# Weights split ahead: an even spread over the feed-forward slots, and 14 more chunks, in a two-layer flow block

## The chip, the cores and the metric

The kernel runs on one core of a Trainium2 chip. The metric is the device time of one execution in microseconds (us); times of runs are given as the median. The core's engines are TensorE (PE, with its weight loads as PEld), VectorE (DVE), ScalarE (ACT), GpSimd (POOL) and SyncE (SP). Each runs its own instructions in order. DMA transfers are issued from the queues of SP, ACT and POOL.

## What is computed

Two layers of a hybrid backbone over 256 context tokens and 256 latent tokens, 1024 channels wide, all in float32. Each layer is a half-step SwiGLU feed-forward network, four token mixers in parallel (a convolution, a gated linear recurrence, a gated delta net, windowed attention), merged by gates and projected, and a second half-step feed-forward network. Only the latent tokens are an output, so the last layer's end runs on the latent half alone.

```python
def swiglu(h, w_gate_up, w_down):
    g, u = jnp.split(h @ w_gate_up, 2, axis=-1)
    return (jax.nn.silu(g) * u) @ w_down
...
# every sub-layer: h = LN(x)*(1+scale)+shift, scale/shift/gate from SiLU(c) @ ada_w
# x <- LayerNorm(alpha*x + w*gate*f(h)),  w = 1/2 for the feed-forward networks
# mixer: z = h @ w_in, four branches, merged = sum(sigmoid(gate_b) * proj_b(y_b)), f = merged @ w_out
```

## The kernel before, in words

**Products in three parts.** Tokens are handled in four tiles of 128 (tiles 0 and 1 context, 2 and 3 latent). A float32 product is made of three PE matmuls, since each operand is split into a rounded part (hi) and a rest (lo): hi by hi (L427), hi by lo (L428), lo by hi (L429), in `mm3`. Weights come in chunks of 128 x 1024 floats (512 KB). `chunk` loads one on SP's queue into `wr` (two buffers), ACT casts it to hi (L123), and DVE or POOL subtracts to get lo (L124; two of three on DVE in a full feed-forward network, all on DVE at the second mixer's end and in the last network). hi and lo go to `wh` and `wl` (three buffers each) or to a named spot: `F`, `Y`, `B` are slots that hold both parts, `G` is four units of 512 columns. `pair` loads two chunks by one transfer (tile `raw`).

**Stages.** In us from the span's start: layer 0 first network about 40 to 440, layer 0 mixer to 1230, layer 0 second network to 1645, layer 1 first network to 2030, layer 1 mixer to about 2545, the norms behind it to 2566, the last network (latent tiles only) to 2749, the last norm and the output to the end at 2766. In what follows the networks are called F0a, F0b, F1a and F1b.

**Fill slots.** `ffn` takes a list `fill`: after most steps of its loops one entry is popped and called, some 25 times in a network; the rest is called ahead of the last stage. Two kinds of work stand in these lists:
- steps of the modulation product (`ada_dot`): a 1 MB load `wa` on SP and four DVE products of 1024 columns (tile `junk`, L203); 28 steps in F0a, 24 in F0b, 12 in F1a;
- weights split ahead (`presplit`): for 38 chunks of the second layer's `w_in`, two halves each: load `C` on SP (L136), cast on ACT (L138), store on ACT's queue, subtraction on DVE (tile `T`, L140), store on POOL's queue (L141). The parts go to a DRAM tile `pre`, and `z_chunk` loads them from there in the mixer, so that the mixer has no cast and no subtraction for them. 14 chunks are done in F0b, 24 in F1a.

`both` lays the two lists over each other, one entry of each to a slot; the shorter gets empty places at its front.

**The second mixer's end.** `mixer` merges the branches, then multiplies by `w_out` (8 chunks, names `wo`; each is used by tile 2 and by tile 3). `SPOT` says where each chunk's parts stand. `fetch` takes chunks 0 to 3 during the merges and 4 to 7 behind the load of `x` from `xspill`. Then each of the two tiles has a chain of two norms: residual (L574, L576), centre (L272, L273, squares on ACT L278, L280), norm (L419, L420), a second centre, ACT L291, PE transposes (L303), modulation, and a split to `h` (L159, L161). F1b's first three pairs of chunks (names `f1`, spots `LAT`) are fetched and split while this goes on.

A scheduler orders the instructions of each engine by priorities and expected times; `issue_after` ties an instruction to follow another.

## Time and profile before

| what | us |
| --- | --- |
| median of three runs | 2767.25 (2759.94 to 2774.62) |
| the profiled execution's own time | 2767.44 |
| its span | 2765.7 |
| PE busy | 2597.6 (94%) |
| DVE busy | 1920.4 (69%) |
| ACT busy | 1094.4 (40%) |
| POOL busy | 883.3 (32%) |

The time is the device's for the whole execution; the span is from the first to the last instruction that the profiler saw, and 1.7 us lie around it. Busy shares are means over the span. An engine's idle time is put down to what ended it.

### The profile page before, as it was taken

The page shows a single profiled execution, that of the slowest core. Times are in us where ns is not written, and L with a number is a line of the kernel's source. Part 1 is how long each engine was busy: PE and PEld are TensorE (multiplying, and loading weights), DVE is VectorE, ACT ScalarE, POOL GpSimd, SP SyncE. Part 2 cuts the span into 40 slices and gives each one's busy share as a digit, 9 for nine tenths or more (in the row PEclk, how much of TensorE's full clock was granted, in tenths as well). Part 3 has the DMA queues.
Part 4 walks back from the last instruction along what each step waited for, and adds up shares of the span by engine and source line. Part 5 has one row for each costly group of instructions (what it writes and reads, how often), then busy time and mean ns, then how long its engine had stood idle before and what let it go on. Part 6 is the DMA issues. An engine that isn't in the chain of part 4 may idle for free.

```text
span 2765.7 us, 38791 instructions
## 1 busy us (share of the span) xinstructions
PE 2597.6 (94%) x14534; PEld 2169.8 (78%) x14534; DVE 1920.4 (69%) x3181; ACT 1094.4 (40%) x2016; POOL 883.3 (32%) x697
## 2 busy tenths in 40 slices
PE   7999999998998999999999989999999989888998
PEld 4877778777776787878778888878887877787897
DVE  4795966678999744266869464758667899756455
ACT  3222245473332533354322353332434534444443
POOL 1323223224545434434233343333210056411221
PEclk9999999999999999999999999999999999999999
DMA  7564633245323433438855449865464754357353
GB/s 268 197 212 154 211 120 104 62 138 168 103 85 96 137 118 124 159 109 312 303 207 191 122 167 329 317 203 171 139 228 136 242 175 149 117 164 257 128 183 107
DMA packets 194779, 477.80 MB, mean 173 GB/s; under 512 B 32816, under 2 KB 72976, under 8 KB 192544
## 3 DMA queue, kind: packets, MB, share of 16 engines
q1 hardware_dynamic: 173216, 424.39, 46.5%
q10 hardware_dynamic: 15264, 30.95, 3.1%
q0 software_dynamic: 6112, 19.99, 1.8%
q8 instruction: 114, 1.87, 0.3%
q14 instruction: 73, 0.60, 0.1%
HBM read 401.82 MB, written 73.45 MB: 172 GB/s over the span
## 4 chain that ended last, share of the span: by engine, by line
PE 32%; DVE 9%; DMA 8%; issue 3%; ACT 3%; POOL 1%; SPq 0%; ACTq 0%; DVEq 0%; POOLq 0%
PE pm L429 9%; PE pm L428 9%; PE pm L427 9%; DMA C<-in_win_dram 4%; DVE junk L203 2%; DVE wl L124 1%; DVE T L140 1%; DMA wr<-in_f_dram 1%; DMA wr<-in_wo_dram 1%; PE pg L921 1%; DMA wa<-in_adaw_dram 1%; PE px L429 1%; PE px L428 1%; PE px L427 1%; DVE G L912 1%
## 5 line engine op out<-in xcount | busy, mean ns | idle before, releaser
L427 PE MATMUL pm<-h,wh 128*128 128x512 f32 (+1 forms) x2512 | 899.9, 360 | 24.9 <-ACT h L159 10.7
L429 PE MATMUL pm<-h,wl 128*128 128x512 f32 (+1 forms) x2512 | 896.4, 357 | 19.4 <-DVE wl L124 18.7
L428 PE MATMUL pm<-h,wh 128*128 128x512 f32 (+1 forms) x2512 | 896.5, 357 | 6.3 <-POOL h L161 6.3
L123 ACT CAST wh<-wr 128x1024 fp32r<-128x1024 f32 x304 | 318.8, 1049 | 621.8 <-DMA wr<-in_f_dram 202.7
L427 PEld LDWEIGHTS pm<-h,wh 128*128 128x128 f32 x2512 | 481.4, 192 | 103.9 <-ACT h L159 12.1
L429 PEld LDWEIGHTS pm<-h,wl 128*128 128x128 f32 x2512 | 481.6, 192 | 98.4 <-DVE wl L124 25.0
L428 PEld LDWEIGHTS pm<-h,wh 128*128 128x128 f32 x2512 | 482.0, 192 | 78.7 <-POOL h L161 8.0
L124 POOL TENSOR_TENSOR wl<-wr,wh 128x1024 fp32r<-128x1024 f32 x108 | 277.4, 2568 | 459.8 <-ACT wh L123 418.6
L124 DVE TENSOR_TENSOR wl<-wr,wh 128x1024 fp32r<-128x1024 f32 x196 | 275.0, 1403 | 209.6 <-ACT wh L123 205.0
L203 DVE SCALAR_TENSOR_TENSOR junk<-wa,cb 128x1024 bf16<-128x1024 f32 x256 | 366.3, 1471 | 10.8 <-DMA wa<-in_adaw_dram 5.7
L161 POOL TENSOR_TENSOR F<-G,F 128x512 fp32r<-128x512 f32 (+1 forms) x94 | 138.0, 1468 | 350.5 <-ACT F L159 336.1
L1155 DVE SCALAR_TENSOR_TENSOR C<-C,vec 128x482 f32<-128x482 f32 (+29 forms) x240 | 173.1, 721 | 4.4 <-ACT C L1147 1.5
L427 PE MATMUL pm<-wh,F 128*128 128x512 f32 x368 | 142.8, 390 | 1.4 <-DVE M L574 1.2
L428 PE MATMUL pm<-wl,F 128*128 128x512 f32 x368 | 143.5, 390 | 0.2 <-POOL wl L124 0.2
L429 PE MATMUL pm<-wh,F 128*128 128x512 f32 x368 | 142.2, 390 | 0.0
L140 DVE TENSOR_TENSOR T<-C,T 128x512 fp32r<-128x512 f32 x76 | 67.1, 883 | 85.7 <-ACT T L138 83.2
L124 DVE TENSOR_TENSOR wl<-raw,wh 128x1024 fp32r<-128x1024 f32 x62 | 76.3, 1232 | 61.6 <-ACT wh L123 61.6
L916 POOL TENSOR_TENSOR wk<-wk,cd 128x512 f32<-128x512 f32 x56 | 72.4, 1295 | 127.8 <-PE pg L938 73.1
L159 ACT CAST F<-G 128x512 fp32r<-128x512 f32 (+1 forms) x94 | 51.0, 543 | 140.0 <-DVE G L441 139.5
L620 DVE SCALAR_TENSOR_TENSOR G<-pm,vec,G 128x506 f32<-128x506 f32 (+5 forms) x126 | 87.4, 694 | 22.3 <-ACT G L615 20.7
L123 ACT CAST wh<-raw 128x1024 fp32r<-128x1024 f32 x64 | 67.1, 1051 | 86.8 <-PE pm L428 40.2
L441 DVE TENSOR_TENSOR G<-G,pm 128x512 f32<-128x512 f32 (+1 forms) x93 | 54.4, 585 | 67.4 <-PE pm L429 63.5
(409 smaller groups left out, 4492.8 us busy)
## 6 DMA issues: line engine op xcount, KB each, us to landing
wr<-in_f_dram SPq DMA_DIRECT2D x204, 512.0 KB, 4.1
wa<-in_adaw_dram SPq DMA_DIRECT2D x64, 1024.0 KB, 5.1
wr<-in_win_dram SPq DMA_DIRECT2D x94, 512.0 KB, 3.6
raw<-in_f_dram SPq DMA_DIRECT2D x30, 1024.0 KB, 5.0
C<-in_win_dram SPq DMA_DIRECT2D x76, 256.0 KB, 4.9
pre<-T ACTq DMA_DIRECT2D x76, 256.0 KB, 4.8
pre<-T POOLq DMA_DIRECT2D x76, 256.0 KB, 5.5
wl<-pre SPq DMA_DIRECT2D x36, 512.0 KB, 5.3
```

Source lines behind the costliest of these rows:

```text
L123: nc.scalar.copy(h, r)
L124: (nc.gpsimd if pool_lo else nc.vector).tensor_sub(l, r, h.bitcast(F32))
L140: nc.vector.tensor_sub(lo, raw, h.bitcast(F32))
L161: eng.tensor_sub(lo, src, hi.bitcast(F32))
L203: nc.vector.scalar_tensor_tensor(junk, w3[:, a], 1.0, self.cb[:, s], op0=ALU.mult, op1=ALU.mult, accum_out=self.modT[l][:, i + a, s:s + 1])
L427: nc.tensor.matmul(ps, wh, xh, start=first, stop=False)
L428: nc.tensor.matmul(ps, wh, xl, start=False, stop=False)
L429: nc.tensor.matmul(ps, wl, xh, start=False, stop=last)
L441: nc.vector.tensor_mul(hf[:, c], sg[:, c], pu[:, c])
L620: nc.vector.scalar_tensor_tensor(acc[:, :, d:], src[:, :, :n - d], w(j), acc[:, :, d:], op0=ALU.mult, op1=ALU.add)
L916: nc.gpsimd.tensor_mul(S(d, n + 1).rearrange("p (h e) -> p h e", h=4), S(d, n).rearrange("p (h e) -> p h e", h=4), gs["cd"][:, d * N_CH + ...
L1155: V.scalar_tensor_tensor(o, x, w(j), o, op0=ALU.mult, op1=ALU.add)
```

## The change

Four things. `both` spreads each list evenly over 25 slots, so a slot gets 0 to 2 modulation steps and 1 to 3 halves. An entry of the split-ahead list is now one half of a chunk (before, a whole chunk); 44 halves are done in F0b (28 before), 60 in F1a (48 before). Each load `C` is tied to come behind the latest `wr` load on SP. And the list has 14 more chunks: the 8 chunks of `w_out` of the second layer and the first 6 of F1b's `f1`. `ready` (which `z_chunk` now calls) loads their parts from DRAM straight into the spots, 1 MB for a chunk in place of the 512 KB of the float32 weights, with no cast and no subtraction. In all 28 halves are added (28 casts, 28 subtractions, 28 loads, 56 stores) and the splits of 14 chunks fall away at the second mixer's end (16 casts and 16 subtractions, since a chunk in `G` has two). F0a's modulation steps, with no split-ahead beside them, are spread by `both` too: three slots get two of them.

```diff
--- before.py
+++ after.py
@@ -44,7 +44,7 @@
 )
 PRE = [Z_GK, Z_GK + 1, Z_GK + 2, Z_GK + 3, Z_AK, Z_AV] + [i for z in (Z_GQ, Z_GV, Z_CG, Z_CA, Z_AQ, Z_LX, Z_LG, Z_GZ)
                                                             for i in range(z, z + 4)]
-PRE_AT = 14
+PRE_AT, SLOTS, N_WO, N_F1 = 44, 25, 8, 3
 LOW = 20000
 SPOT = ("F", "F", "G", "G", "Y", "Y", "B", None)
 LAT = ((None, None), ("F", "F"), ("F", None))
@@ -104,7 +104,7 @@
         self.n_ck += 1
         if raw is None:
             raw = self.sb.tile([P, 1024], F32, tag="wr", bufs=2, name="wr")
-            nc.sync.dma_start(raw, src)
+            self.fetched = nc.sync.dma_start(raw, src).ins
         elif isinstance(raw, str):
             raw = self.slot(raw, name="raw")[:, :1024]
             nc.sync.dma_start(raw, src)
@@ -124,28 +124,33 @@
             (nc.gpsimd if pool_lo else nc.vector).tensor_sub(l, r, h.bitcast(F32))
         return hi, lo
 
-    def presplit(self, l, i):
-        nc = self.nc
-        dst = self.dr.tile([P, 2048], F32, name=f"pre{l}_{i}")
-        self.pre[l, i] = dst
-
-        def go():
-            for k in range(2):
-                c = slice(k * 512, (k + 1) * 512)
-                raw = self.unit("C")
-                nc.sync.dma_start(raw, self.t["win"][l, i][:, c])
-                h, lo = self.T(F32R), self.T(F32R)
-                nc.scalar.copy(h, raw)
-                nc.scalar.dma_start(dst[:, c], h.bitcast(F32))
-                nc.vector.tensor_sub(lo, raw, h.bitcast(F32))
-                nc.gpsimd.dma_start(dst[:, 1024 + k * 512:1024 + (k + 1) * 512], lo.bitcast(F32))
-
-        return go
-
-    def z_chunk(self, l, i, at=None, raw=None):
-        if (l, i) not in self.pre:
-            return self.chunk(self.t["win"][l, i], at=at, raw=raw)
-        nc, src = self.nc, self.pre[l, i]
+    def presplit(self, key, src):
+        nc = self.nc
+        dst = self.dr.tile([P, 2048], F32, name="pre" + "_".join(str(k) for k in key))
+
+        def go(k):
+            c = slice(k * 512, (k + 1) * 512)
+            raw = self.unit("C")
+            with self.tc.issue_after(self.fetched):
+                nc.sync.dma_start(raw, src[:, c])
+            h, lo = self.T(F32R), self.T(F32R)
+            nc.scalar.copy(h, raw)
+            nc.scalar.dma_start(dst[:, c], h.bitcast(F32))
+            nc.vector.tensor_sub(lo, raw, h.bitcast(F32))
+            nc.gpsimd.dma_start(dst[:, 1024 + k * 512:1024 + (k + 1) * 512], lo.bitcast(F32))
+            self.pre[key] = dst
+
+        return [lambda k=k: go(k) for k in range(2)]
+
+    def ready(self, key, src, at=None, raw=None):
+        if key not in self.pre:
+            return self.chunk(src, at=at, raw=raw)
+        nc, src = self.nc, self.pre[key]
+        if at == "G":
+            hl = [self.G(F32R) for _ in range(4)]
+            for k in range(4):
+                nc.sync.dma_start(hl[k].bitcast(F32), src[:, k * 512:(k + 1) * 512])
+            return hl[:2], hl[2:]
         if at:
             w = self.slot(at, F32R, name="w" + at)
             nc.sync.dma_start(w.bitcast(F32), src)
@@ -154,6 +159,9 @@
         nc.sync.dma_start(hi.bitcast(F32), src[:, :1024])
         nc.sync.dma_start(lo.bitcast(F32), src[:, 1024:])
         return hi, lo
+
+    def z_chunk(self, l, i, at=None, raw=None):
+        return self.ready(("win", l, i), self.t["win"][l, i], at, raw)
 
     def split(self, hi, lo, src, pool_lo=True):
         self.last = self.nc.scalar.copy(hi, src).ins
@@ -460,7 +468,9 @@
         self.ju = lambda: self.unit("C")
         chunk = self.chunk
 
-        def two(src, at=(None, None)):
+        def two(src, at=(None, None), key=None):
+            if key and key + (0,) in self.pre:
+                return [self.ready(key + (a,), src[a], at[a]) for a in range(2)]
             if lat:
                 return self.pair(src, "Y", at)
             return [chunk(src[a], at[a]) for a in range(2)]
@@ -473,7 +483,7 @@
                 at = LAT if lat else ((None, None), (None, "Y"), ("Y", "F"))
                 ws = start or []
                 for i in range(0 if start else nh):
-                    ws.append(two(self.t["f1"][l, f, 2 * (m0 + i):2 * (m0 + i) + 2], at[i]))
+                    ws.append(two(self.t["f1"][l, f, 2 * (m0 + i):2 * (m0 + i) + 2], at[i], ("f1", l, f, i)))
                 hid.append((self.F(F32R), self.F(F32R)))
                 for g in groups:
                     if lat:
@@ -1378,7 +1388,7 @@
 
         def fetch(n0, n1):
             for n in range(n0, n1):
-                ws[n] = self.chunk(self.t["wo"][l, n // 4, n % 4], at=spots[n])
+                ws[n] = self.ready(("wo", l, n), self.t["wo"][l, n // 4, n % 4], spots[n])
 
         def conv_out():
             y[0] = self.new_y()
@@ -1480,12 +1490,16 @@
             return box, after
 
         def both(ada, pre):
-            n = max(len(ada), len(pre))
-            ada, pre = ([None] * (n - len(x)) + list(x) for x in (ada, pre))
-            return [lambda fs=fs: [f() for f in fs if f] for fs in zip(ada, pre)]
+            n = SLOTS
+            ada, pre = ([fs[len(fs) * i // n:len(fs) * (i + 1) // n] for i in range(n)] for fs in (ada, pre))
+            return [lambda fs=x + y: [f() for f in fs] for x, y in zip(ada, pre)]
 
         every = (0, 1, 2, 3)
-        pre = [self.presplit(1, i) for i in PRE]
+        L = DEPTH - 1
+        pre = [(("win", L, i), self.t["win"][L, i]) for i in PRE]
+        pre += [(("wo", L, n), self.t["wo"][L, n // 4, n % 4]) for n in range(N_WO)]
+        pre += [(("f1", L, 1, m, a), self.t["f1"][L, 1, 2 * m + a]) for m in range(N_F1) for a in range(2)]
+        pre = [f for k, x in pre for f in self.presplit(k, x)]
         for l in range(DEPTH):
             last = l == DEPTH - 1
 
```

On SP's queue in F0b, at the list's start, loads stand in this order before (`C` is a half to be split ahead, `wr` a chunk that the network needs, `wa` a modulation step's weights):

```order
L136 DMA C<-in_win_dram 128x512
L107 DMA wr<-in_f_dram 128x1024
L136 DMA C<-in_win_dram 128x512
L107 DMA wr<-in_f_dram 128x1024 x3
L136 DMA C<-in_win_dram 128x512 x6
L107 DMA wr<-in_f_dram 128x1024
L136 DMA C<-in_win_dram 128x512 x2
```

and now, from the same transfer of the gate rows on:

```order
L107 DMA wr<-in_f_dram 128x1024 x4
L135 DMA C<-in_win_dram 128x512 x2
L107 DMA wr<-in_f_dram 128x1024 x2
L135 DMA C<-in_win_dram 128x512 x2
L207 DMA wa<-in_adaw_dram 128x2x1024
L107 DMA wr<-in_f_dram 128x1024
L207 DMA wa<-in_adaw_dram 128x2x1024 x2
L107 DMA wr<-in_f_dram 128x1024
```

Before, up to six halves stand in a row there, and now two or three stand behind a `wr`.

On SP's queue at the second mixer's end, from the last two loads ahead of `x`, before:

```order
L107 DMA wr<-in_wo_dram 128x1024
L1423 DMA x<-xspill 128x2048
L107 DMA wr<-in_wo_dram 128x1024 x2
L98 DMA raw<-in_f_dram 128x2x1024
L107 DMA wr<-in_wo_dram 128x1024 x2
L107 DMA wr<-in_f_dram 128x1024 x2
L98 DMA raw<-in_f_dram 128x2x1024 x3
```

and now (`prewo_4` is chunk 4 of `w_out` with both parts, `pref_1_1_0_0` the first chunk of F1b):

```order
L1433 DMA x<-xspill 128x2048
L156 DMA wY<-prewo_4_398 128x2048
L107 DMA wr<-in_f_dram 128x1024
L156 DMA wF<-pref_1_1_1_0_404 128x2048
L156 DMA wY<-prewo_5_399 128x2048
L159 DMA wh<-prewo_7_401 128x1024
L160 DMA wl<-prewo_7_401 128x1024
L98 DMA raw<-in_f_dram 128x2x1024
L159 DMA wh<-pref_1_1_0_0_402 128x1024
L160 DMA wl<-pref_1_1_0_0_402 128x1024
L159 DMA wh<-pref_1_1_0_1_403 128x1024
L156 DMA wB<-prewo_6_400 128x2048
```

Behind `x` there were four chunks of `w_out` (2 MB) with one pair of `f1` (1 MB) between them; now chunk 6 (`wB`) stands behind 7.5 MB of other loads, 8.5 MB from `x` to its own end (the row of `wl` of `pref_1_1_0_1`, 512 KB, stands ahead of it too and is left out here as it repeats).

On DVE at the same place, from the split of chunk 6 to the first norm of tile 2, before:

```order
L124 TENSOR_TENSOR wB<-wr,wB 128x1024
L124 TENSOR_TENSOR wl<-wr,wh 128x1024
L574 TENSOR_TENSOR M<-pm,gate 128x512
L124 TENSOR_TENSOR wl<-raw,wh 128x1024 x2
L576 SCALAR_TENSOR_TENSOR x,sum<-x,M 128x512
L574 TENSOR_TENSOR M<-pm,gate 128x512
L576 SCALAR_TENSOR_TENSOR x,sum<-x,M 128x512
L272 TENSOR_SCALAR ns<-sum 128x1
L273 TENSOR_SCALAR nm<-sum 128x1
L419 SCALAR_TENSOR_TENSOR M<-x,nm,norm_g 128x512 x2
L124 TENSOR_TENSOR wF<-raw,wF 128x1024 x2
L280 TENSOR_SCALAR v<-var 128x1
```

and now:

```order
L584 TENSOR_TENSOR M<-pm,gate 128x512
L586 SCALAR_TENSOR_TENSOR x,sum<-x,M 128x512
L584 TENSOR_TENSOR M<-pm,gate 128x512
L586 SCALAR_TENSOR_TENSOR x,sum<-x,M 128x512
L280 TENSOR_SCALAR ns<-sum 128x1
L281 TENSOR_SCALAR nm<-sum 128x1
L427 SCALAR_TENSOR_TENSOR M<-x,nm,norm_g 128x512 x2
L288 TENSOR_SCALAR v<-var 128x1
```

The subtractions L124 are gone from the norms' chain. (Lines of the kernel after are 8 to 14 higher from here on.) On PE the products by `w_out` are reordered: of the 96 matmuls on the two tiles, the 24 with chunks 6 and 7 stood at two places before (12 in the middle, 12 at the end) and are now the last 24.

## Rows read from the trace of the kernel before

**Rows 1.** The page, part 1: busy us of each engine, share, instructions.
```profile
PE 2597.6 (94%) x14534; PEld 2169.8 (78%) x14534; DVE 1920.4 (69%) x3181; ACT 1094.4 (40%) x2016; POOL 883.3 (32%) x697
```

**Rows 2.** Busy by stretch: us, PE, PEld, DVE, ACT, POOL, PEclk, DMA share, GB/s.
```profile
1250.00:1605.00 355.00, 350.38 (x1591) 286.98 (x1591) 265.93 (x371) 114.46 (x165) 114.50 (x80) 1.00 0.63 218
1645.00:1965.00 320.00, 317.26 (x1428) 259.23 (x1427) 200.03 (x260) 111.87 (x153) 112.55 (x92) 1.00 0.72 246
2545.00:2566.00 21.00, 5.95 (x25) 4.35 (x23) 13.65 (x38) 14.71 (x30) 6.09 (x8) 0.59 0.67 247
```

**Rows 3.** PE's waits in 1250 to 1605 (F0b): total us, times, longest.
```profile
PE pm L429 <- DVE wl L124: 4.2, 4, 1.8
```

**Rows 4.** PE's waits in 1645 to 1965 (F1a).
```profile
PE pm L427 <- DVE M L574: 1.2, 1, 1.2
PE pm L429 <- DVE wl L124: 0.8, 2, 0.5
PE pm L427 <- ACT wh L123: 0.7, 1, 0.7
```

**Rows 5.** PE's waits in 50 to 400 (F0a).
```profile
PE pm L429 <- DVE wl L124: 6.3, 4, 2.8
```

**Rows 6.** PE's waits in 2500 to 2566 (the second mixer's end).
```profile
PE pg L303 <- ACT T L291: 12.7, 2, 9.4
PE pm L427 <- ACT wh L123: 1.8, 2, 1.1
```

**Rows 7.** The page, part 5: split-ahead's subtraction on DVE, its busy and idle time.
```profile
L140 DVE TENSOR_TENSOR T<-C,T 128x512 fp32r<-128x512 f32 x76 | 67.1, 883 | 85.7 <-ACT T L138 83.2
```

**Rows 8.** Groups by line in 1640 to 1820: split-ahead's cast on ACT.
```profile
L138 ACT CAST T<-C 128x512 fp32r<-128x512 f32 x47 | 29.2, 621 | 78.8 <-DMA C<-in_win_dram 73.4 <-DVE T L140 2.5 <-DVE M L574 2.0
```

**Rows 9.** DVE's busy time by stretch in F0b: us, DVE, PEclk, DMA share, GB/s.
```profile
1360.00:1400.00 40.00, 40.00 (x53) 0.96 0.78 276
1440.00:1480.00 40.00, 26.29 (x34) 1.00 0.44 150
```

**Rows 10.** DVE's timeline in F0a: start, us, instruction.
```profile
178.56 1.21 DVE L203 SCALAR_TENSOR_TENSOR junk<-wa,cb 128x1024 bf16<-128x1024 f32 x1
179.70 3.42 DVE L203 SCALAR_TENSOR_TENSOR junk<-wa,cb 128x1024 bf16<-128x1024 f32 x1
```

**Rows 11.** DVE's timeline at the norms behind the second mixer.
```profile
2542.53 2.36 DVE L124 TENSOR_TENSOR wF<-raw,wF 128x1024 fp32r<-128x1024 f32 x2 [0.59 <-ACT wF L123]
...
2548.57 1.22 DVE L124 TENSOR_TENSOR wF<-raw,wF 128x1024 fp32r<-128x1024 f32 x1
...
2550.32 1.23 DVE L124 TENSOR_TENSOR wl<-raw,wh 128x1024 fp32r<-128x1024 f32 x1
2551.45 0.69 DVE L576 SCALAR_TENSOR_TENSOR x<-x,M 128x512 f32<-128x512 f32 x1
```

**Rows 12.** PE's timeline at the same place, [idle before <-releaser].
```profile
2545.34 0.39 PE L428 MATMUL pm<-wl,F 128*128 128x512 f32 x1
2545.57 0.39 PE L429 MATMUL pm<-wh,F 128*128 128x512 f32 x1
2555.31 1.97 PE L303 MATMUL pg<-ident,T 128*128 128x128 f32 x8 [9.35 <-ACT T L291]
2560.64 1.97 PE L303 MATMUL pg<-ident,T 128*128 128x128 f32 x8 [3.36 <-ACT T L291]
```

**Rows 13.** SP's timeline at the same place: issue of the load of `x`.
```profile
2515.49 0.33 SPq L1423 DMA_DIRECT2D x<-xspill  x1
```

**Rows 14.** DMA issues in 2512 to 2548: KB each, us to landing.
```profile
x<-xspill SPq DMA_DIRECT2D x1, 1024.0 KB, 6.0
```

**Rows 15.** Busy by stretch, columns as in rows 2: what the DMA moved.
```profile
20.00:30.00 10.00, 6.53 (x44) 4.01 (x37) 5.46 (x8) 6.15 (x8) 3.41 (x2) 0.66 1.02 419
2515.00:2525.00 10.00, 10.00 (x81) 9.78 (x81) 5.35 (x7) 4.92 (x8) 1.43 (x2) 1.00 0.89 323
```

**Rows 16.** Tile C's users, split-ahead's subtraction: ns min/median/max, first and last start us.
```profile
L140 DVE TENSOR_TENSOR T<-C,T x76: 677/693/3144, 1245.2 to 1816.8; 128x512 fp32r<-128x512 f32 x76
```

## The prediction

> **What bounds the kernel now.** I read the busy shares first. PE is busy 94% of the span, DVE 69%, the others under half [rows 1]. So the question for every edit is whether PE waits less or more, and not how much work DVE or ACT gains. Next I read the stretches that the change touches, one by one. In F0b PE is busy 350.4 of 355 us, in F1a 317.3 of 320; only behind the second mixer is it idle, 15 of 21 us [rows 2]. Then I read what ended PE's waits in each. In F0b it was DVE's lo part of a weight, 4.2 us in four waits [rows 3]; in F1a three small causes, 2.7 us in all [rows 4]; in F0a the lo part again, 6.3 us [rows 5]. At the mixer's end ACT's cast of a weight cost 1.8 us and the norms' ACT L291 12.7 us [rows 6]. Thus all the waits that the change could remove are 4.2 + 2.7 + 6.3 + 1.8 + 12.7 = 27.7 us, and of the last term only a part, since a norm must follow its sums in any case. 0.5% of the time, about what a measurement of this kernel can tell from no change, is 13.8 us.
>
> **F0a.** Only modulation steps move. Three slots get two of them, eight DVE products in a row at 1.21 us or more [rows 10], some 10 us, and the last stage has fewer ahead of it. The waits there total 6.3 us, the longest 2.8 [rows 5]. A gain can't exceed 6.3; three doubled slots, each with one wait like the longest, would lose 8.4. With both signs open I take 0.
>
> **F0b.** Sixteen halves are added. A half is 0.88 us of DVE [rows 7] and 0.62 us of ACT [rows 8], so DVE gains 14 and ACT 10 us in 355, of which they have 89 and 241 free [rows 2]. The free time is uneven: DVE is full in one stretch of 40 us and has 14 us free in another [rows 9]. An even spread should remove part of the 4.2 us that PE waits for DVE's lo parts. Bounds: -4.2, when all of it goes; +14, when every added subtraction stood ahead of a split that PE waits for. I take -1, near the lower end, because DVE stays under 80% in the mean.
>
> **F1a.** Twelve halves are added, 10.6 us of DVE, with 120 us free there. Modulation steps now start in the first slots. The waits are 2.7 us [rows 4]. Bounds -2.7 and +10.6; I take -1. The loads, 0.25 MB a half, and their two stores have to fit on the DMA too. Its share is 0.72 here [rows 2], and the 12 halves add 3 MB read and 6 MB written to 320 us at 246 GB/s (79 MB): a tenth or so more. I count them at nothing, covered by the share that is free; if the cover were gone, the extra 9 MB at the 419 GB/s of [rows 15] would be 23 us of DMA.
>
> **The order behind `wr`.** The tie of `C` to the latest `wr` makes a weight that PE needs land earlier, and `C` later. What is queued behind `C` is ACT: it already waits 1.6 us for each half (78.8 for 47, [rows 8]), with casts `wh` behind it, while PE in F1a waited 0.7 us for those casts. I price this at 0; the bound is below, with the rivals.
>
> **The merges.** In place of chunk loads through `wr` and casts of them on ACT and DVE, chunks 0 to 3 of `w_out` go straight to their spots. Two PE waits for casts, 1.8 us [rows 6], should go, since fewer chunks pass the two `wr` buffers there: -1.8 (bounds -1.8 and 0).
>
> **The norms behind the mixer.** Six subtractions of `f1` halves lie in DVE's queue between the norms' steps. The four of them that stand in [rows 11] take 2.36 + 1.22 + 1.23 = 4.8 us, and the ACT casts ahead of them hold the squares up as well. For tile 3, whose split `h` the first matmul of F1b needs, I follow the chain: the last product starts at 2545.57 and ends at about 2546.0 [rows 12], but the residual's last sum starts only at 2551.45, behind L420 of tile 2, the splits and its own neighbours [rows 11]; from its end, 2552.1, to the transposes at 2560.64 are 8.5 us. Without the splits the two residuals and two sums follow the product at once: 2546.0 and three steps of 0.69 us, the length of L576 [rows 11], make 2548.1. Then 8.5 us more give 2556.6. But the last product of tile 2 is later than before, since chunks 6 and 7 are now the last 24 of the 96 matmuls: it ends 12 matmuls, 2.8 us at 0.23 us each [rows 12], ahead of tile 3's. The two chains now run through ACT and DVE nearly together, and I add 1.4 us, two more such steps, for it. That puts the transposes at 2558.0: -2.6 (bounds -4.8, all the splits; 0, when the chains collide for as long).
>
> **Chunk 6's load.** This is the cost. `x` is issued at 2515.49 and lands 6.0 us later, at 2521.5 [rows 13, 14]. Behind it stand 8.5 MB up to the end of `wB`, in order. At 419 GB/s, which the queue reached at the start [rows 15], a MB (1,048,576 bytes) takes 2.5 us, so `wB` lands at 2521.5 + 21.3 = 2542.8, some 2543.3 with its semaphore. PE wants it 23 matmuls ahead of the last: 2545.57 - 23 x 0.23 = 2540.3. That is a new wait of 3 us. Its bounds are 0 (some of the loads are issued ahead of `x`'s landing by other room, since the merges use less of the DMA) and, at the 323 GB/s that the stretch itself moved [rows 15], 3.25 us a MB, 27.6 us, a landing at 2549.6 with the semaphore: +9. I take +3, the bandwidth that a full queue has shown, because the row of 323 holds issue gaps of SP. Behind the wait stand both tiles' last sums, so all of it moves the norms.
>
> The Trainium skill ("DMA: Bandwidth & Descriptors", section "Specifications") gives about 358 GB/s as what HBM yields to one core. The row of 419 GB/s is above that, so the trace disagrees for that stretch. By the page a MB would take 2.9 us, the wait would be 6.5, and the sum would be about zero.
>
> **The sum.** 0 - 1 - 1 - 1.8 - 2.6 + 3 = -3.4 us. From the profiled execution's own 2767.4 (1.7 above its span, 0.2 above the median of the runs) this gives 2764.0. The bounds add to -6.3 - 4.2 - 2.7 - 1.8 - 4.8 = -19.8, 2748, and on the other side, terms of unlike places taken singly, to rival 3 below.
>
> **Rivals.** *1. All touched waits go.* The spread removes the lo waits of three networks, 6.3 + 4.2 + 2.7 us, the merges' 1.8 and the norms' 2.6, and `wB` comes in time: -17.6, 2749.8. For it: the lo waits are four single events in each of two networks [rows 3, 5], as a burst of work ahead of them would make. Against: in F0a three slots become longer, and DVE gains work in the other two.
>
> *2. Nothing shows.* PE is at 99% in F1a and F0b, so what is moved under it is hidden either way, and at the mixer's end the chain's gain is given back by `wB` and the reordered products: 2767. The spread may also not do what it says, since the scheduler had already set loads and subtractions by its own priorities. For it: the last half was split at 1816.8 [rows 16], while F1a runs to 1965, so the bunched work harmed PE for 2.7 us at most.
>
> *3. Slower: the added halves fill DVE's queue.* DVE works in order, and each half holds it 0.88 us and costs up to 1.13 us of idling for its cast (85.7 over 76, [rows 7]): 2.0 us, 56 for the 28. Where DVE is full [rows 9] this goes on to the lo parts behind it, and to PE. It decides from a third on: 19 us, less the 4.4 gained at the mixer's end (1.8 + 2.6) and plus the 3 of `wB`, give 2785. Against: DVE has 26 to 37% free in these networks. For: one `junk` took 3.42 us beside another's 1.21 [rows 10], and halves take 0.88 in the mean, so DVE's steps do stretch.
>
> The Trainium skill ("SBUF — State Buffer", section "SBUF: two separate sides") says that a DVE operation with two SBUF inputs and a GpSimd operation that reads SBUF lock each other out for a whole instruction. That fits the 3.42 us, and it speaks against this change, which adds 28 such subtractions beside POOL's own. By it the sum would move only through rival 3, whose price does not rest on the rule.
>
> *4. `wB` at the slower rate,* +9 in place of +3: 2770.
>
> **How the numbers follow.** Chances: the forecast 0.42, rival 1 0.20, rival 2 0.18, rival 3 0.12, rival 4 0.08. Faster than 2753.4 is most of rival 1 and a little of the forecast: 0.21. Slower than 2781.1 is rival 3 and a little of 4: 0.14. Within is the rest, 0.65. The range has to leave out no more than 2 in 10: it reaches to rival 1 below, 2748, and above past rivals 2 and 4 and part of the way to 3, 2779. The forecast's own range is 2756 to 2771.
>
> **What would show it.** In the changed profile, F0b and F1a should have PE waits for `wl` of some 3 and 2 us, and DVE busy up by 14 and 11 us. The two waits for casts near 2507 should be gone. No L124 should stand between L280 and L428 of tile 2 (lines of the kernel after). The last 24 products by `w_out` should begin behind a wait for the load of `wB` of about 3 us, and the gap ahead of the first transposes should be shorter than 9.35 us. If there is no wait for `wB`, the forecast is 3 us too high. If PE waits for `wl`, or for a cast behind `C`, by 10 us or more in a network, rival 3 is the case. If the waits in F0a, F0b and F1a all fall under 1 us, it is rival 1.

## The result: slower by 1.2%

The changed kernel takes 2801.1 us (median of 4 runs, 2791.8 to 2803.8), the kernel before 2769.3 (4 runs). The ratio is 1.0119, with a 95% interval of 1.0099 to 1.0138: 32 us slower by the medians and 33 by the ratio, where 2764 was forecast. The profiled execution has a span of 2801.4 us, 35.7 more than before.

The page of the changed kernel, part 1, answers to [rows 1]:

```profile
PE 2610.4 (93%) x14534; PEld 2171.2 (78%) x14534; DVE 1929.1 (69%) x3193; ACT 1095.9 (39%) x2028; POOL 898.7 (32%) x725
```

PE does the same 14534 matmuls, and the others' busy time hardly moves (DVE +9, ACT +2, POOL +15 us). So the loss is not work that the others gained. PE's own busy time grew by 12.8 us for the same matmuls, and its idle time by 22.9: it waits, and some of its matmuls run longer. The busy time by stretch (columns as in [rows 2]) says where:

```profile
1250.00:1605.00 355.00, 337.03 (x1521) 273.31 (x1520) 265.10 (x346) 113.35 (x156) 116.31 (x93) 0.99 0.75 256
1645.00:1965.00 320.00, 307.42 (x1418) 252.11 (x1417) 197.74 (x253) 118.69 (x173) 119.06 (x106) 0.98 0.78 266
2545.00:2600.00 55.00, 38.52 (x194) 32.17 (x193) 20.57 (x53) 17.45 (x39) 8.54 (x11) 0.83 0.80 314
```

In F0b PE is busy 337 of 355 us (350 before), in F1a 307 of 320 (317 before). Stages drift as time is lost, so from here on they are cut by PE's own work: the time between the starts of the k-th and the m-th of PE's 14534 matmuls. F0b is from 6000 to 7700, F1a from 7700 to 9600, the second mixer's end with its norms from 12450 to 13210, F0a from 0 to 1780.

| stage, us | before | after | difference | forecast |
| --- | --- | --- | --- | --- |
| F0a | 406.6 | 407.4 | +0.8 | 0 |
| F0b | 369.1 | 386.3 | +17.1 | -1 |
| F1a | 409.8 | 424.1 | +14.3 | -1 |
| the second mixer's end | 129.6 | 132.1 | +2.5 | -1.4 |

So 31.4 of the 35.7 us by which the two profiled executions differ were lost in the two networks whose spread was to help. Of the 31.4, PE's idle time makes 22.2 (16.2 before, 38.4 after, summed over the gaps between its matmuls). The other 9.2 lie outside these gaps; about half of them is PE's clock, as is shown below.

PE's waits in F0b after (total us, times, longest), which answer to [rows 3]:

```profile
PE pm L437 <- DVE wl L124: 10.8, 6, 2.7
PE pm L435 <- DVE M L584: 2.1, 2, 1.8
PE pm L436 <- POOL wl L124: 1.9, 1, 1.9
PE pm L436 <- DVE wl L124: 1.4, 2, 0.7
```

and in 1645 to 2010 (F1a), beside [rows 4] (before, this longer window has one wait more, 1.4 us for POOL's part of `h`):

```profile
PE pm L435 <- ACT G L447: 3.6, 3, 2.4
PE pm L435 <- ACT h L167: 3.0, 1, 3.0
PE pm L436 <- POOL wl L124: 2.5, 2, 1.6
PE pm L435 <- DVE M L584: 2.3, 1, 2.3
```

In F0b DVE's lo parts are late, 12.2 us where it was 4.2. In F1a it is no one engine: the ACT step L447, POOL's lo parts, DVE's residual. (The wait for `h`, 3.0, stands in the norms between the networks before too.) ACT's timeline in F1a shows how a step of ACT comes late:

```profile
1945.14 0.62 ACT L137 CAST T<-C 128x512 fp32r<-128x512 f32 x1 [4.44 <-DMA C<-in_f_dram]
...
1946.22 0.62 ACT L137 CAST T<-C 128x512 fp32r<-128x512 f32 x1 [0.45 <-ACT T L137]
...
1950.58 0.62 ACT L137 CAST T<-C 128x512 fp32r<-128x512 f32 x1 [3.73 <-DMA C<-in_f_dram]
1951.10 1.04 ACT L123 CAST wh<-wr 128x1024 fp32r<-128x1024 f32 x1
...
1952.05 0.59 ACT L447 ACTIVATE G<-pm 128x512 f32<-128x512 f32 x1
```

ACT stands at L137 until a half `C` has landed. Behind it stand the cast of a weight and L447, which frees PE's result buffer. PE's wait of 2.4 us for L447 began at about 1950.3, in this very gap. DVE's subtractions then wait for ACT (76.7 us in 1645 to 2010, 64.6 before), and POOL's stores for DVE. Over the stages as cut above, ACT's idle time ahead of the casts of halves rose from 34.4 to 65.9 us in F0b and from 78.8 to 121.5 in F1a.

### The profile page after: what moved, and what is told of

Same layout as the page of the kernel before. It is cut to its first block, busy times and chain, and to the rows that moved or that the text cites. A ratio compares the mean times of both kernels' runs of the same rounds, so it can differ in the third digit from the quotient of the medians.

```text
span 2801.4 us, 39004 instructions
## 1 busy us (share of the span) xinstructions
PE 2610.4 (93%) x14534; PEld 2171.2 (78%) x14534; DVE 1929.1 (69%) x3193; ACT 1095.9 (39%) x2028; POOL 898.7 (32%) x725
## 5 line engine op out<-in xcount | busy, mean ns | idle before, releaser
L435 PE MATMUL pm<-h,wh 128*128 128x512 f32 (+1 forms) x2512 | 899.7, 360 | 30.9 <-ACT h L167 10.7
L435 PEld LDWEIGHTS pm<-h,wh 128*128 128x128 f32 x2512 | 480.6, 192 | 111.8 <-issue 13.4
L436 PEld LDWEIGHTS pm<-h,wh 128*128 128x128 f32 x2512 | 480.7, 191 | 76.7 <-POOL h L169 5.8
L124 POOL TENSOR_TENSOR wl<-wr,wh 128x1024 fp32r<-128x1024 f32 x108 | 277.6, 2570 | 412.8 <-ACT wh L123 387.7
L124 DVE TENSOR_TENSOR wl<-wr,wh 128x1024 fp32r<-128x1024 f32 x195 | 270.8, 1389 | 198.1 <-ACT wh L123 197.7
L211 DVE SCALAR_TENSOR_TENSOR junk<-wa,cb 128x1024 bf16<-128x1024 f32 x256 | 370.7, 1487 | 10.9 <-DMA wa<-in_adaw_dram 6.9
L139 DVE TENSOR_TENSOR T<-C,T 128x512 fp32r<-128x512 f32 x104 | 92.1, 892 | 114.6 <-ACT T L137 113.5
L137 ACT CAST T<-C 128x512 fp32r<-128x512 f32 x104 | 64.4, 619 | 187.4 <-DMA C<-in_win_dram 96.9
L124 DVE TENSOR_TENSOR wl<-raw,wh 128x1024 fp32r<-128x1024 f32 x59 | 72.7, 1233 | 62.1 <-ACT wh L123 62.1
L140 POOL DMA_DIRECT2D prewin<-T x76 | 42.0, 552 | 207.3 <-DVE T L139 191.3
```

The costliest lines, as they stand in the source:

```text
L124: (nc.gpsimd if pool_lo else nc.vector).tensor_sub(l, r, h.bitcast(F32))
L137: nc.scalar.copy(h, raw)
L139: nc.vector.tensor_sub(lo, raw, h.bitcast(F32))
L211: nc.vector.scalar_tensor_tensor(junk, w3[:, a], 1.0, self.cb[:, s], op0=ALU.mult, op1=ALU.mult, accum_out=self.modT[l][:, i + a, s:s + 1])
L435: nc.tensor.matmul(ps, wh, xh, start=first, stop=False)
L436: nc.tensor.matmul(ps, wh, xl, start=False, stop=False)
```

## The experiments

Eighteen kernels were run, each beside the kernel before on the same chip (f4 by a single run). Beside the ratio stand the differences of the stages from the kernel before, in us, read from one execution each. A stage that a kernel leaves alone differs by up to 7 us too (F0b in h3), so that a single stage is good to no better than that. The profiled execution need not be a median one either: g0's is 10 us below its median, h3's 9 above. The verdicts rest on the ratios.

| kernel | ratio (95%) | F0a | F0b | F1a | mixer's end |
| --- | --- | --- | --- | --- | --- |
| the change | 1.0119 (1.0099 to 1.0138) | +0.8 | +17.1 | +14.3 | +2.5 |
| e1: no tie | 1.0092 (1.0062 to 1.0121) | -0.3 | +9.8 | +6.2 | +1.8 |
| e2: spread only | 1.0036 (1.0022 to 1.0050) | -1.0 | +1.3 | +6.0 | -0.2 |
| e3: more chunks only | 1.0119 (1.0095 to 1.0142) | +1.6 | +8.9 | +10.4 | +3.7 |
| e5: tie only | 1.0056 (1.0037 to 1.0075) | +0.8 | +7.7 | +3.9 | +3.0 |
| e4: spread and tie | 1.0003 (0.9992 to 1.0015) | +0.5 | +1.1 | -0.6 | +5.6 |
| f1: no subtraction | 1.0063 (1.0040 to 1.0085) | -1.7 | +4.6 | +7.2 | +6.0 |
| f2: no load | 1.0034 (1.0018 to 1.0050) | -1.2 | +3.9 | +2.7 | +1.9 |
| f3: store from ACT | 1.0090 (1.0068 to 1.0111) | +1.2 | +14.4 | +12.1 | +1.4 |
| f4: no stores | one run | -0.7 | +7.6 | +0.3 | |
| g0: halves, unread | 1.0088 (1.0064 to 1.0112) | -2.2 | +5.4 | +13.0 | -0.2 |
| g1: traffic, issued as in a half | 1.0100 (1.0077 to 1.0122) | +0.7 | +10.9 | +13.4 | -1.6 |
| g2: compute only | 1.0053 (1.0035 to 1.0072) | +0.7 | +5.9 | +4.0 | -0.3 |
| g4: the change, wB split | 1.0089 (1.0071 to 1.0106) | -1.7 | +16.6 | +11.4 | -7.3 |
| h1: 26 halves in F0a | 1.0085 (1.0066 to 1.0103) | +13.9 | +4.5 | +0.6 | -4.8 |
| h2: copies, at the start | 1.0206 (1.0190 to 1.0221) | +16.4 | +4.5 | +12.5 | -0.6 |
| h3: 12 halves in F0a | 1.0057 (1.0035 to 1.0079) | +6.9 | +6.6 | +3.1 | -1.2 |
| h4: no tie, wB split | 1.0073 (1.0056 to 1.0091) | -2.6 | +11.5 | +2.7 | -6.0 |
| k1: copies, in place | 1.0110 (1.0081 to 1.0139) | +0.5 | +2.0 | +25.6 | +2.6 |

**The three parts apart (e1 to e5).** My theory after the first reading was that the tie does it: `C` lands late, and ACT and DVE stand for it. The rivals were the number of halves, and the spread. e1 takes the tie away:

```diff
             raw = self.unit("C")
-            with self.tc.issue_after(self.fetched):
-                nc.sync.dma_start(raw, src[:, c])
+            nc.sync.dma_start(raw, src[:, c])
```

e2 has the spread alone, e3 the 14 chunks alone, e5 the tie alone, e4 spread and tie without the chunks. The fewer chunks (e2, e4, e5), and the old list (e3, e5):

```diff
-PRE_AT, SLOTS, N_WO, N_F1 = 44, 25, 8, 3
+PRE_AT, SLOTS, N_WO, N_F1 = 28, 25, 0, 0
...
-            n = SLOTS
-            ada, pre = ([fs[len(fs) * i // n:len(fs) * (i + 1) // n] for i in range(n)] for fs in (ada, pre))
-            return [lambda fs=x + y: [f() for f in fs] for x, y in zip(ada, pre)]
+            pre = [lambda fs=pre[i:i + 2]: [f() for f in fs] for i in range(0, len(pre), 2)]
+            n = max(len(ada), len(pre))
+            ada, pre = ([None] * (n - len(x)) + list(x) for x in (ada, pre))
+            return [lambda fs=fs: [f() for f in fs if f] for fs in zip(ada, pre)]
```

> The change without the tie of the loads C to the latest wr load; spread and 14 more chunks stay. Late loads: ACT and DVE stand behind C only because of the tie, so the 16 us lost in F0b and the 17 us lost in F1a go, and 0 to 5 us over before remain: 2768 to 2775. Amount: the 28 added halves are the load, 25 to 33 us over before remain: 2793 to 2803. Spread: the halves that now stand in the late slots are the load, the same 2793 to 2803.

> The kernel before with the even spread alone: 76 halves (28 in F0b), no tie, no further chunks. Spread: 20 to 30 us over before, 2790 to 2800, with waits of PE in the last third of F0b and F1a. Late loads and amount: within 5 us of before, 2765 to 2774.

> The kernel before with the 14 further chunks alone: 104 halves, whole chunks packed into the last slots as before, no tie. Amount: 20 to 33 us over before, 2790 to 2802. Late loads and spread: the networks lose under 5 us, and the mixer's end is as in the change, so 2766 to 2776.

> The kernel before with the tie alone: 76 halves in whole chunks, packed into the last slots, but each load C behind the latest wr. Late loads: 15 to 30 us over before, 2784 to 2800, with ACT idle for C ahead of casts that PE waits for. Amount and spread: within 5 us of before, 2765 to 2774.

> The change without the 14 further chunks: spread and tie with the 76 halves of before. If the three parts add as measured alone (10 and 15 us): 2785 to 2795. If the spread undoes what the tie costs: 2768 to 2778. If the 28 further halves are the decisive part of the change: at least 15 us below the change, 2786 or less.

As the whole cause, the tie fell. The chunks alone cost as much as the whole change (1.0119 both; 11 of e3's 33 us have a cause of their own, told under "One event"), and without them spread and tie together cost nothing (1.0003). So it is the added chunks, on top of spread and tie, that make the change slow, and by the stages it is their halves in F0b and F1a. The tie alone and the spread alone do cost 15 and 10 us, so the parts don't add: the spread undoes what the tie costs at 76 halves, and at 104 the tie adds some 8 us to the spread (e1 to the change; their intervals overlap, so this is likely and not shown).

For F0b the traces say more. Over the stage, PE waits for DVE's lo parts 12.2 us in the change, 10.7 in e1 and 9.4 in e3, which all have the added halves, but 4.6 in e4, which has not (4.2 before). ACT's idle time ahead of the casts of halves is nearly as long in e4 as in the change (58.8 and 65.9 us; 34.4 before), and e4 loses 1.1 us there. So that ACT stands for a load does not cost by itself; it can where a step that PE needs stands behind, as L447 above.

**What in a half costs (f1 to f4, on the change).** f1 leaves out DVE's subtraction, f2 the load, f3 issues the lo part's store from ACT, f4 leaves out both stores (there nothing is read back, so the table gives the networks alone). In this order, without the lines that only follow from these:

```diff
-            nc.vector.tensor_sub(lo, raw, h.bitcast(F32))
-            nc.gpsimd.dma_start(dst[:, 1024 + k * 512:1024 + (k + 1) * 512], lo.bitcast(F32))
+            nc.gpsimd.dma_start(dst[:, 1024 + k * 512:1024 + (k + 1) * 512], h.bitcast(F32))
```

```diff
-            raw = self.unit("C")
-            with self.tc.issue_after(self.fetched):
-                nc.sync.dma_start(raw, src[:, c])
+            raw = self.ident.unsqueeze(1).to_broadcast([P, 4, P])
```

```diff
-            nc.gpsimd.dma_start(dst[:, 1024 + k * 512:1024 + (k + 1) * 512], lo.bitcast(F32))
+            nc.scalar.dma_start(dst[:, 1024 + k * 512:1024 + (k + 1) * 512], lo.bitcast(F32))
```

```diff
-            nc.scalar.dma_start(dst[:, c], h.bitcast(F32))
...
-            nc.gpsimd.dma_start(dst[:, 1024 + k * 512:1024 + (k + 1) * 512], lo.bitcast(F32))
-            self.pre[key] = dst
```

> The change with the split-ahead subtraction on DVE left out for all 104 halves (the hi part is stored twice, so the outputs are not the reference's). DVE's queue as the cause: F0b and F1a together lose under 5 us against before in place of 31, and the time is 2765 to 2775. DMA as the cause: the traffic is the same and 25 us or more of the 31 stay, 2793 or more. ACT waiting for C: 20 us or more stay.

> The change with the loads C left out: every half is split from a tile that is always there (so the outputs are not the reference's); casts, subtractions and stores stay. Late loads as the cause: F0b and F1a together lose under 8 us, 2768 to 2778, since ACT never stands waiting for C. DVE's queue as the cause: 20 to 31 us stay, 2788 to 2801. DMA as the cause: a third of the added traffic goes, 20 us stay.

> The change with the lo part's store issued on ACT's queue and not on POOL's. POOL's queue as the cause (its splits stand behind a store that waits for DVE): the loss falls by 8 us or more, 2793 or less. DVE, DMA or late loads as the cause: within 5 us of the change, 2796 to 2806, or slower, since ACT then waits for DVE.

> The change with both stores of each half left out; the second mixer then splits all its chunks itself, so only F0b and F1a are compared. DMA as the cause: they lose under 10 us against before in place of 31. DVE's queue or late loads as the cause: 25 us or more stay.

Leaving out one of the three gives back most of the 31.4 us of F0b and F1a: 19.6 without the subtraction (11.8 remain), 24.8 without the load, 23.5 without the stores (a single run). They sum to twice what there is to give back, so they are no separate shares of one loss. I read it so: a half is a chain through SP, ACT, DVE and POOL, and whichever link is taken out loosens all of it. f3 leaves POOL's queue open. Its loss is 8 us less by the ratio, the least that I had expected if POOL's store held up the splits behind it, but 1.0090 and 1.0119 have intervals that overlap, 26.5 of the 31.4 us stay in its two networks, and ACT, in POOL's place, now waits for DVE.

**Traffic or work (g0 to g2, h2, k1, on the kernel before).** g0 adds the 28 halves whole, but nobody reads them. In g1 an added half is only loaded and stored twice; in g2 only cast and subtracted, from a tile that is always there; in k1 it is two DRAM-to-DRAM copies, which wait for nothing (h2 has the same without the tie, one of the two on POOL's queue). The main lines of g1, g2 and k1 for an added half:

```diff
+                nc.sync.dma_start(raw, src[:, c])
+                nc.scalar.dma_start(dst[:, c], raw)
+                nc.gpsimd.dma_start(dst[:, 1024 + k * 512:1024 + (k + 1) * 512], raw)
```

```diff
+                nc.scalar.copy(r4(h), raw)
+                nc.vector.tensor_sub(r4(lo), raw, r4(h.bitcast(F32)))
```

```diff
+                for o in (k * 512, 1024 + k * 512):
+                    with self.tc.issue_after(self.fetched):
+                        nc.sync.dma_start(dst[:, o:o + 512], src[:, c])
```

> The kernel before with 28 further halves (16 in F0b, 12 in F1a), complete with load, cast, subtraction and stores, whose parts nobody reads: the second mixer and its end stay as before. No tie, no even spread. If the networks alone carry the loss: 15 to 25 us over before, 2780 to 2790. If the loss comes from reading the parts back at the mixer's end: within 5 us of before.

> As g0_both, but the 28 further halves are only loaded and stored twice, with no cast and no subtraction. DMA as the cause: 12 to 25 us over before, like g0_both. Queues of ACT and DVE as the cause: within 5 us of before. A coupling of both: under half of g0_both.

> As g0_both, but the 28 further halves are only cast on ACT and subtracted on DVE, from a tile that is always there, with no load and no store. DVE's queue as the cause: 12 to 25 us over before, like g0_both. DMA as the cause: within 4 us of before. A coupling of both: under half of g0_both.

> As g1_traffic, but the traffic of the 28 further halves is made by copies from DRAM to DRAM (two of 256 KB for each half, one from POOL's queue and one from SP's), which need no tile and wait for nothing. DMA traffic as the cause: F0b and F1a lose 12 us or more against before, 2780 to 2795. Queues that stand waiting for a load or a store as the cause: under 6 us, 2765 to 2775.

> As h2_copies, whose copies ran at the very start and so told nothing of F0b and F1a: now the copies are issued from SP behind the latest wr load, 32 of them among F0b's weight loads, 24 in a row late in F1a. Only traffic is added, and nothing waits for it. DMA traffic itself as the cause: F0b loses 8 us or more against before. Queues that stand waiting, as the cause: F0b loses under 4 us. F1a's row of 6 MB at once may delay the weights behind it by some 15 us once, in either case.

g0 costs 24 us by its ratio. Its profiled execution holds 16, with 18.4 in the two networks and nothing at the mixer's end: the loss is made in the networks. g1, meant to be traffic alone, costs as much, but it did not test that: its store on ACT's queue waits for the load, and ACT's waits in F0b and F1a hold 17.1 and 26.1 us of casts `wh` behind a load `C`. h2 failed as a test too: with nothing to wait for, its copies ran in the first 77 us. k1 put them in place. Its copies in F0b were spread over 83 us (tile `prewo`, first and last start, and us to landing):

```profile
L136 SPq DMA_DIRECT2D prewo<-in_wo_dram x32: 496/596/605, 1457.1 to 1540.2; - x32
...
DMA to landing us min/median/max: 3.9/5.7/6.8
```

These 32 copies read and write 8.4 MB each, more than the 16 halves' 4.2 read and 8.4 written, and F0b lost 2.0 us, where the change lost 17.1. So traffic as such is not what the change lost there by. (Against g0's 5.4 the difference is within what one stage is good to.) In F1a the 24 copies stood in a row on SP, and PE's waits in 1930 to 1990 show what that does to the weight behind them:

```profile
PE pm L439 <- ACT wY L123: 11.5, 1, 11.5
```

Work alone (g2) costs 15 us, +5.9 in F0b, as much as g0's +5.4 there. In F1a g0 lost 13.0 and g2 4.0, but that column compares something else in these kernels, as follows.

**One event.** e3, g0, g1, g2 and h2 all lose 11.0 to 11.7 us at the same place late in F1a, matmuls 9100 to 9400 (k1, whose weight is late there as well, 23.9), and h2 has no half added there. What the six share is the old `both` with a longer list: 30 pairs in F1a in place of 24. As `both` sets the shorter list's empty places at its front, the modulation steps start later, and the entries past the 25 or so slots are called in one go. The kernels without the tie that have not this list (e1, e2, h1, h3, h4) lose -0.2 to 1.2 us there. Tile `junk`, whose products are these steps, before and in h2, from 1640 us on:

```profile
L203 DVE SCALAR_TENSOR_TENSOR junk<-wa,cb x48: 1211/1218/3437, 1738.9 to 1915.4; 128x1024 bf16<-128x1024 f32 x48
L214 DVE SCALAR_TENSOR_TENSOR junk<-wa,cb x48: 1209/1215/3419, 1911.2 to 1994.5; 128x1024 bf16<-128x1024 f32 x48
```

48 products stand in 83 us where it was 176, and so they do in all six. This is 11 us of e3's loss too, and the F1a column of these six does not tell what a half costs. The change has no such row of products, as its spread lays them over 245 us; what it loses at that place, 12.3, holds the wait for L447 shown above and one of 1.6 us for POOL's lo part. In g0 DVE's and POOL's timelines at the event read, one behind the other:

```profile
1957.05 1.22 DVE L210 SCALAR_TENSOR_TENSOR junk<-wa,cb 128x1024 bf16<-128x1024 f32 x1
1958.19 0.08 DVE L210 DVE_READ_ACCUMULATOR junk<-wa,cb 128x1 f32 x1
1958.19 3.36 DVE L124 TENSOR_TENSOR wl<-wr,wh 128x1024 fp32r<-128x1024 f32 x1
```

```profile
1957.37 3.10 POOL L124 TENSOR_TENSOR wY<-wr,wY 128x1024 fp32r<-128x1024 f32 x1 [3.63 <-ACT wY L123]
```

DVE's subtraction takes 3.36 us while POOL's runs, where alone it takes 1.22 [rows 11]. Ahead of it stand eleven products `junk`, the first of 3.41 us, with one other split among them. PE waits 3.10 us for it. Then PE's stretches of 2 us (us, PE busy, granted clock, DMA share, GB/s):

```profile
1956.00:1958.00 2.00, 2.00 (x10) 1.00 0.00 0
1958.00:1960.00 2.00, 0.50 (x3) 1.00 0.00 0
1960.00:1962.00 2.00, 0.40 (x2) 1.00 0.00 0
1962.00:1964.00 2.00, 2.00 (x7) 0.61 0.66 172
1964.00:1966.00 2.00, 2.00 (x6) 0.53 0.86 352
1966.00:1968.00 2.00, 2.00 (x10) 1.00 0.21 67
```

After the gap the granted clock is 0.53 to 0.61 for 4 us, and 13 matmuls run in place of 20: at 0.23 us each the wait of 3 us costs some 1.6 more. The lower clock is about half of the other 9.2 us of the change: F0b and F1a stand at the lower clock for 28.4 us there, for 19.1 before, and 9.3 us more at half speed are 4.7. Some 3 more, by my estimate, are lost at the gaps' edges: the change has 19 gaps more, and at each the matmul ahead, 0.39 us long, is not overlapped by one that starts 0.23 us after it [rows 12]. The rest is not accounted for. The Trainium skill ("SBUF — State Buffer", section "SBUF: two separate sides") says that such DVE and GpSimd operations exclude each other for a whole instruction; 3.36 beside 3.10 us agrees, as DVE's ends 1.1 us after POOL's.

**Another place for the halves (h1, h3).** Thirteen chunks (all but wB), or the six of `f1`, split ahead in F0a, with before's lists for the rest:

```diff
-        pre += [(("wo", L, n), self.t["wo"][L, n // 4, n % 4]) for n in range(N_WO)]
+        add = [(("wo", L, n), self.t["wo"][L, n // 4, n % 4]) for n in range(N_WO) if n != 6]
...
-                          + A(l, 2, 0) + A(l, 2, 2), pre[PRE_AT:] if last else []), after,
+                          + A(l, 2, 0) + A(l, 2, 2), pre[PRE_AT:] if last else add), after,
```

> The kernel before with its own 76 halves where they were, no tie; 13 of the 14 further chunks (not wB) are split ahead in F0a, where nothing was split ahead, one half or two to a slot. If the loss is what a half costs wherever it is put: F0a loses 15 to 20 us, the mixer's end gains 7 to 10, 2776 to 2784. If it is that F0b and F1a were full already: F0a loses under 5 us, and the time is 2762 to 2768, at or below before.

> As h1_in_F0a with the 6 chunks of f1 alone, 12 halves. If halves cost 1.1 us each wherever they are: F0a loses 13 us, the norms gain 4 to 5, 2774 to 2778. If F0a has room: 2762 to 2767, under before by the norms' gain.

F0a lost 13.9 us for 26 halves and 6.9 for 12: 0.53 and 0.57 us a half. F0b, without the tie, lost 8.9 (e3) and 9.8 (e1) for 16: 0.56 and 0.61. So a half costs about the same in these two, and there was no room in the network without split-ahead either. (h3's figure alone would not show it: its F0b, left alone, lost 6.6 too.) F1a is not told: e1's 6.2 for 12 halves is no more than the 6.0 that the spread alone lost there (e2).

**The mixer's end (g4, h4).** Chunk 6 is loaded as float32 and split, as before:

```diff
-        if key not in self.pre:
+        if key not in self.pre or key[0] == "wo" and key[2] == 6:
```

> The change with chunk 6 of w_out (wB) not read in parts but loaded as float32 and split as before. If the direct load of wB is what the mixer's end loses by: the wait for wB of 2.5 us and what follows it go, and the time falls by 3 to 5 us against the change, 2796 to 2798. If the order of the products is: within 2 us of the change, 2799 to 2803.

> The change without the tie and with chunk 6 loaded as float32 and split as before. If the two gains add (8 to 12 from the tie, 10 from wB): 2779 to 2783. If they are one and the same: 2789 to 2791.

In the change wB was issued at 2559.91; tile `wB` landed so long after:

```profile
L156 SPq DMA_DIRECT2D wB<-prewo x1: 319/319/319, 2559.9 to 2559.9; - x1
...
DMA to landing us min/median/max: 13.4/13.4/13.4
```

PE's timeline and its stretches there:

```profile
2573.31 0.50 PE L435 MATMUL pm<-wB,F 128*128 128x512 f32 x1 [2.46 <-DMA wB<-prewo]
...
2589.02 1.97 PE L311 MATMUL pg<-ident,T 128*128 128x128 f32 x8 [8.33 <-ACT T L299]
```

```profile
2565.00:2570.00 5.00, 5.00 (x23) 1.00 1.02 416
2570.00:2573.00 3.00, 0.85 (x4) 1.00 1.00 421
2573.00:2575.00 2.00, 1.69 (x7) 0.95 1.02 426
2575.00:2577.00 2.00, 2.00 (x7) 0.50 0.98 408
```

The DMA is full, 408 to 426 GB/s, PE waits 2.46 us, and again the clock falls to 0.50, the lower of its two levels. In g4, with wB split, the same gap reads

```profile
2575.21 1.97 PE L311 MATMUL pg<-ident,T 128*128 128x128 f32 x8 [5.11 <-ACT T L299]
```

with no wait in the products. The end is 7.3 us shorter than before and 9.8 shorter than in the change; the whole time falls from 1.0119 to 1.0089, with intervals that overlap. Of the 9.8, 4.3 lie at the products by `wB` themselves (the wait of 2.46, and the lower clock behind it) and 3.2 in the gap ahead of the transposes (8.33 to 5.11). Another 2.2 lie before matmul 12660, where no product by `w_out` has begun, and are not put down to `wB`. In h4 the missing tie and the split wB together give 1.0073: its end is 6.0 us shorter than before, but F0b and F1a still lose 14.2. No version with added halves beat the kernel before.

## Why the prediction was wrong

**The step that failed** is the cost of the halves in F0b and F1a, -1 and -1, measured +17.1 and +14.3. I set their DVE and ACT time against free time in the mean (89 and 120 us of DVE) and took values near the lower bounds. The busy time came out about as counted (over the stages as cut above, DVE +14.1 us in F0b and +7.3 in F1a, forecast 14 and 11); the waiting did not: PE's gaps in the two grew from 16.2 to 38.4 us. The upper bounds, +14 and +10.6, were too low as well: they priced DVE's own time, and a half also puts a load ahead of what ACT does next and, through PE's waits, costs PE's clock. Rival 3, given 0.12, had the right sign and, for F0b, the mechanism: PE's waits for DVE's lo parts there reach 12.2 us, over the 10 that I had named as its sign. In F1a they make 1.7, and there it was not the mechanism. Its "a third on", 19 of 56 us, was 31, and DVE is only one link: without the load as much came back as without the subtraction.

**The order behind `wr`**, priced at 0, is some 8 us at 104 halves (1.0119 against e1's 1.0092, intervals that overlap), 15 alone (e5) and none at 76 halves with the spread (e4). I named what stands behind `C`, ACT's casts, and took PE's 0.7 us of waits before as proof that it does no harm; with `C` later it did. (The 78.8 us for 47 halves that I read there are 1.7 us each, not 1.6.)

**Traffic** at nothing was right for F0b, as far as one execution tells (k1: +2.0).

**F0a** at 0 was right (+0.8), though I had left both signs open, so that it tests little.

**The merges**: -1.8 forecast. The two waits for casts are gone: at matmul 12960 the changed kernel is 32.65 us behind, at 12980 30.33, a gain of 2.3. (Over the whole way from 12450 it is 0.9, since 1.5 were lost ahead of 12660.)

**Chunk 6's load**: the landing was worked out at 419 GB/s and the DMA ran at 416 to 426; the wait of 3 us came as 2.46, behind a landing at 2573.3, forecast 2543.3 in a stage that now runs 30.3 us later. But the term was mis-sized all the same: against g4 it cost up to 7.5 us, 4.3 at the products and 3.2 in the gap behind them. Two things were left out: the clock behind the wait, and the order of the products, which puts chunks 6 and 7 last for both tiles and brings the two chains of norms together. g4 differs in both, so whether the 3.2 come from the late load or from the order stays open.

**The norms**: -2.6 forecast. The gap ahead of the transposes fell by 1.0 us in the change (9.35 to 8.33) and by 4.2 in g4. So the gain is there when the products by chunk 6 come early, and in the change most of it was lost again.

Right were, then, the places and signs of the mixer's end; its sum, -1.4 against +2.5, is off by less than one stage is good to and small beside the networks' error.

**What stays open**: how the 31.4 us are shared among load, cast, subtraction and store, since they don't add; how much of the change's loss in F1a is the added halves and how much the spread's new order (e2 lost 6.0 us there with nothing added, e4 nothing); whether more buffers for `C` would free ACT, which was not tried.

## What to carry to other kernels

Free time of an engine in the mean does not make added work free when PE has no slack: here each half of 0.6 us on ACT and 0.9 on DVE cost PE some 0.55 us in two networks (h1, e3), and 1.1 in the change, where its load is tied late as well. A step that waits for a load holds up what stands behind it on its engine, as L137 did on ACT. When a list grows past its slots, look where its tail goes: it cost 11 us in five of these kernels, whatever was in the list. Work moved ahead pays only if the place that it leaves gives back more: 7.3 us at the most at the mixer's end, against 16 to 31. And when a load replaces a load plus a split, count from when its destination must be free and what stands ahead of it in the queue: the split that was saved took some 2 us, and the products by the later chunk cost 4.3 more.

## What the runs showed of the hardware

At the two places shown, gaps of 2.46 and 3.10 us on PE are followed, within 2 us of their end, by stretches of 2 to 4 us at a granted clock of 0.50 to 0.61, so that a short wait can cost more than its length. It need not: behind a gap of 2.50 us in g0, at 1405 to 1408 us, the clock stays 1.00 up to 1416. A subtraction on DVE that met one on POOL took 3.36 us in place of 1.22. And the DMA held 406 to 426 GB/s for 16 us at the mixer's end (2565 to 2581 us), as much as in the first stretch of [rows 15].
